# Seven block products for eight in a down projection, with sums of weights made in device memory

## The chip, the cores and the metric

The kernel runs on one core of one Trainium2 chip. The metric is the device time of one execution in microseconds (us). Before the change the median of three runs is 1150.55 us (1149.58 to 1152.34).

## The reference

One decoder layer is applied to a prompt of 512 rows and to 8 samples of 8 rows, 576 columns in the kernel's transposed layout. Model width is 1024. In order: a half-step feed-forward layer, a mixer (a recurrent branch and a pooling branch), cross attention over 256 memory tokens, a second half-step feed-forward layer, a final norm. All is float32. The part that changes is the second feed-forward step:

```python
def swiglu(x, w_gate, w_up, w_down):
    return (jax.nn.silu(x @ w_gate) * (x @ w_up)) @ w_down

x = x + 0.5 * swiglu(rmsnorm(x, p['ffn2_norm']), p['ffn2_w_gate'], p['ffn2_w_up'], p['ffn2_w_down'])
```

The hidden width is 2816, that is 22 chunks of 128.

## The kernel before

Activations are kept transposed: `x` is a tile of 128 partitions, 8 panels (the 1024 model channels) and 576 columns, cut in two halves of HT = 288 columns. It stays in SBUF from the first step to the last.

**Precision.** Each float32 operand is split into a high part (a cast to fp32r on ACT, line 144) and a low part (source minus high part on DVE, line 145). A product is three matmuls, high by high, high by low, low by high (`mm3`, line 159). With 128 x 128 weights and 288 columns each matmul is one entry of line 132 in the profile.

**Gate and up.** The function `ffn` (line 331) makes both steps. The first chunks of hidden channels (3 in step one, 2 in step two, `STD`) are plain products (`std`). For each further chunk f the gate and up weights and the two column halves are treated as 2 x 2 blocks and multiplied in the Strassen-Winograd way: seven products (named 11, E, 22, F, G, 12, H) for eight, with sums of the weights (DVE, lines 407, 408, 409, 420), sums of the activations made once (`HalfNorm.sums`, `last`), and sums of the results gathered in PSUM, with copies of partial results by ACT (lines 585, 589, 599). Each such product is 12 matmuls. Weights are loaded two chunks ahead (`load`, line 389) into a ring of four raw tiles (tag "wr"), and split in `prepare_a` and `prepare_b` into a ring of five (tags "wh", "wl").

**Hidden values.** A finished chunk of hidden values is split into `hh`, `hl` (lines 572 to 576), in groups of 4, 4, 4, 5, 5 chunks (`FGS`).

**Down.** While the chunks of one group are made, the down projection of the group before is worked off: `down` (line 448) puts steps in a queue, one for each output panel j and chunk k, six matmuls each (2 halves x 3). After each of the seven products of a chunk, `fill` (line 564) takes about 1.1 steps from the queue. When a panel's last chunk is done, DVE adds the PSUM tile to `x` (line 464). The down weights come in panels through the same ring "wr" and are split by `make` (line 436). The last group has no products left to lie beside: it runs as a tail, with columns cut 320 and 256 (`TAIL`, lines 653 to 676), and the final norm follows panel by panel.

**Order.** The order of the matmuls of both steps is written out by hand: inside the PSUM pool "ff" each matmul gets an edge to the one before (lines 130 to 138). The order of ACT, DVE, POOL and the DMA queue of SP is a planner's: it takes the instruction that comes first in the text among those it reckons to be ready. So the Silu of line 611 starts at 1041.50 us in the trace and the cast to "wh_g" at 1043.03, though the latter stands first in the text. On the chip each engine then runs its list in that order.

**PSUM.** "u" has two banks, "c" and "a" one each, "d" two tiles of two banks, which the down projection uses.

Of the kernel before, what the change touches and what calls it, by code (L numbers as in the profile page):

```python
# [9 lines left out]
F32 = mybir.dt.float32  # L10
# [6 lines left out]
P = 128  # L17
# [5 lines left out]
FGS = (4, 4, 4, 5, 5)  # L23
STD = (3, 2)
TAIL = ((0, 320), (320, T))
WARM = 11
# [39 lines left out]
def hybrid_step(ctx, tc, a):  # L66
# [60 lines left out]

    chain = [None]

    def mm(*args, **kw):  # L130

        i = te.matmul(*args, **kw)  # L132
        if "ff" in now:
# [4 lines left out]
        return i  # L138


# [189 lines left out]

    def ffn(name, n, fp, turn, plain, head=False):

        wstd, wgu, wd = a[f"{name}_s"], a[f"{name}_gu"], a[f"{name}_d"]

# [6 lines left out]
        def small_tile(nm_):  # L341
            return fp.tile([P, HT], F32, tag="pc", bufs=3, name=nm_)

        def full_tile(nm_):
            return fp.tile([P, T], F32, tag="e", bufs=2, name=nm_)

# [29 lines left out]
        def std_out(i, pg, pu):  # L376
            e = full_tile("e")
            for (p, q), (_, rr) in zip(pieces(pg, e), pieces(pg, r)):
                v.tensor_mul(q, p, rr)
            s.activation(e, e, AF.Silu, scale=-1.0)  # L380
            v.tensor_mul(e, e, half)
            for p, q in pieces(pu, e):
                v.scalar_tensor_tensor(out=q, in0=p, scalar=-1.0, in1=q, op0=ALU.mult, op1=ALU.mult)
            split(hh[0][:, i, :], hl[0][:, i, :], e)

# [36 lines left out]


        steps = deque()
        panels = [(gi, j) for gi in range(len(FGS)) for j in range(DC)]
        fetched, wdown = {}, {}

        def fetch(i):

            if i < len(panels) and i not in fetched:  # L430
                gi, j = panels[i]
                c0, fg = sum(FGS[:gi]), FGS[gi]
                fetched[i] = wp.tile([P, fg, P], F32, tag="wr", bufs=WRB, name=f"wr_d{j}")
                nc.sync.dma_start(fetched[i], wd[j, :, c0:c0 + fg, :])

        def make(i, pool=None):

            if i < len(panels) and i not in wdown:
                fetch(i)
                gi, j = panels[i]  # L440
                if pool is None:
                    w = [fp.tile([P, FGS[gi], P], F32R, tag=tag, bufs=2, name=f"{tag}{j}") for tag in ("dh", "dl")]
                else:
                    w = [pool.tile([P, FGS[gi], P], F32R, name=f"t{q}{j}") for q in "hl"]
                split(*w, fetched[i])
                wdown[i] = w

        def down(gi, after=None):

            fg = FGS[gi]  # L450
            h_, l_ = hh[gi], hl[gi]
            pd = {}

            def step(j, k):
                i = gi * DC + j
                if k == 0:
                    make(i)
                    make(i + 1)
                    fetch(i + 2)
                    pd[j] = dual("pd")  # L460
                mm3([pd[j][:, h, :HT] for h in range(2)], [q[:, k, :] for q in wdown[i]],
                    [[q[:, k, h * HT:(h + 1) * HT] for h in range(2)] for q in (h_, l_)], k == 0, k == fg - 1)
                if k == fg - 1:
                    v.tensor_add(halves(x[:, j, :]), pd[j][:, :, :HT], halves(x[:, j, :]))  # L464
                    if after:
                        after(j)

            steps.extend((step, j, k) for j in range(DC) for k in range(fg))

        def go(m):  # L470
            for _ in range(min(m, len(steps))):
                q, *at = steps.popleft()
                q(*at)

# [5 lines left out]

        group(0)
        ts = [fp.tile([P, 2, 3, HT], F32, tag=tag, bufs=2, name=f"t_{tag}") for tag in ("hh", "hl")]

# [53 lines left out]
        for i in range(3):  # L537
            s.copy(r[:, i * third:(i + 1) * third], free[i][:, HT:HT + third])
        half = fp.tile([P, T], F32, name=f"half_{n.name}")
        s.activation(half, r, AF.Copy, scale=0.5)  # L540
        std(cols(ps1[1]), w, range(4, DC))
        std_out(0, *ps0)
        load(plain)
        if plain > 2:
# [11 lines left out]
        load(plain + 1)  # L556
        prepare_b(plain)

# [5 lines left out]
        def fill():  # L564
            nonlocal pace
            if gi:
                pace += per_slot
                m = min(int(pace), len(steps))
                pace -= int(pace)
                go(m)  # L570

        def finish_chunk(c):
            w, U, g, h_, l_ = c
            product(U, w["22"], n, T4, False)
            v.tensor_mul(g[:, :HT], U, g[:, :HT])
            split(h_, l_, g)

        for f in range(plain, FFC):
            if f - g0 == FGS[gi]:
                g0, gi = f, gi + 1  # L580
                group(gi)
            w = W.pop(f)
            U, C, A = (single(tag, f"p{tag}")[:, :HT] for tag in "uca")
            product(U, w["11"], n, N11, True)
            s.copy(A, U)
            fill()
# [6 lines left out]
            if f == g0:  # L593
                down(gi - 1)
            prepare_a(f + 1)
            fill()
            product(U, w["F"], n, T2, False)
            u2 = small_tile("u2")
            s.copy(u2, U)
            fill()  # L600
# [3 lines left out]
            v.tensor_mul(g[:, HT:], g[:, HT:], r[:, HT:])  # L604
            fill()
            prepare_b(f + 1)
            if f == plain:
                n.last(0, ts[0][:, :, 0, :])
            product(A, w["12"], n, N21, False)
            v.tensor_mul(g[:, :HT], A, r[:, :HT])  # L610
            s.activation(g, g, AF.Silu, scale=-1.0)
            v.tensor_mul(g, g, half)
            fill()
# [3 lines left out]
            load(f + 2)  # L617
            if f == plain:
                n.last(1, ts[1][:, :, 0, :])
            if f == FGS[0] - 1:  # L620
                make(0)
                fetch(1)
            fill()
            before = w, U, g, hh[gi][:, f - g0, :], hl[gi][:, f - g0, :]
        finish_chunk(before)
        after = turn()
        if after:
# [3 lines left out]

        fg = FGS[-1]
        tp = now["tail"]
# [19 lines left out]
        for c0, c1 in TAIL:  # L653
            for j in range(DC):
                pd = single("u", "pd") if j % 2 else dual("pd")[:, 0, :]
                po = pd[:, :c1 - c0]
                for k in range(fg):
                    mm3([po], [q[:, k, :] for q in ws[j]], [[q[:, k, c0:c1]] for q in (hh[gi], hl[gi])],
                        k == 0, k == fg - 1)
                y = x[:, j, c0:c1]  # L660
                v.tensor_add(y, po, y)
                if j == 0:
# [32 lines left out]
    if True:  # L695
# [67 lines left out]
        def proj(kind, c):  # L763
            base = {"l": 0, "g": LC, "p": 2 * LC}[kind]
            ps[kind, c] = bank(f"in_{kind}{c}")
            project(ps[kind, c], panel(a["w_in"][base + c], DC, P, "i"), nm.xx)

        def lru_in(c):
# [407 lines left out]

    ffn("f2", n2, begin("f2", side="right"), to_tail, STD[1])
    end("f2", "tail", "ff")
# [10 lines left out]
def _inputs(i):  # L1189
# [43 lines left out]
    for n in (1, 2):  # L1233
# [5 lines left out]
        out[f"f{n}_gu"] = gu.reshape(FFC - m, P, 4, KP, P)[:, :, [3, 0, 1, 2]]  # L1239
        out[f"f{n}_d"] = panels(l0[f"ffn{n}_w_down"])  # L1240
    out["w_in"] = panels(l0["w_in"])
# [48 lines left out]
```

## Time and profile before

| what | value |
|---|---|
| median of three runs | 1150.55 us |
| the profiled execution's own time | 1148.76 us |
| its span | 1146.7 us |
| granted TensorE clock over the span | 0.997 |
| PE busy | 1129.4 us, 98% |
| DVE busy | 835.0 us, 73% |
| ACT busy | 544.0 us, 47% |
| POOL busy | 24.1 us, 2% |
| data moved | 126.30 MB, mean 110 GB/s |

The span runs from the first to the last instruction of the profiled execution; its own time holds what lies around the span too. Busy time of PE is to be read with care, since matmuls are pipelined; in the loops the interval from one matmul's start to the next is the better measure. An engine's idle time costs something only where the chain that ends last runs through it. The second step's chunk loop begins a little before 770 us and ends near 1098 us, the tail follows.

### The profile page before, as it was taken

The page shows a single profiled execution, that of the slowest core. Times are in us where ns is not written, and L with a number is a line of the kernel's source. Part 1 is how long each engine was busy: PE and PEld are TensorE (multiplying, and loading weights), DVE is VectorE, ACT ScalarE, POOL GpSimd, SP SyncE. Part 2 cuts the span into 40 slices and gives each one's busy share as a digit, 9 for nine tenths or more (in the row PEclk, how much of TensorE's full clock was granted, in tenths as well). Part 3 has the DMA queues.
Part 4 walks back from the last instruction along what each step waited for, and adds up shares of the span by engine and source line. Part 5 has one row for each costly group of instructions (what it writes and reads, how often), then busy time and mean ns, then how long its engine had stood idle before and what let it go on. Part 6 is the DMA issues. An engine that isn't in the chain of part 4 may idle for free.

```text
span 1146.7 us, 20764 instructions
## 1 busy us (share of the span) xinstructions
PE 1129.4 (98%) x8634; PEld 1113.0 (97%) x8634; DVE 835.0 (73%) x1335; ACT 544.0 (47%) x852; POOL 24.1 (2%) x47
## 2 busy tenths in 40 slices
PE   8999999999999999999999999999999999999996
PEld 8999999999999999999998879999999999999996
DVE  8887787788774788977634566769877877877664
ACT  8644344444432555875622564545443443443343
POOL 0000000000000022110000000000000000000000
PEclk9999999999999999999999999999999999999998
DMA  8223233233221352232655753212333332332212
GB/s 294 94 83 110 75 93 101 83 95 115 80 81 51 116 177 60 71 128 87 224 199 181 281 201 93 74 37 84 93 93 91 94 92 75 106 104 72 88 47 83
DMA packets 44285, 126.30 MB, mean 110 GB/s; under 512 B 4832, under 2 KB 9952, under 8 KB 44064
## 3 DMA queue, kind: packets, MB, share of 16 engines
q1 hardware_dynamic: 41808, 122.84, 34.4%
q10 hardware_dynamic: 2384, 2.15, 0.6%
q8 instruction: 67, 1.10, 0.4%
q14 instruction: 26, 0.21, 0.1%
HBM read 120.16 MB, written 4.81 MB: 109 GB/s over the span
## 4 chain that ended last, share of the span: by engine, by line
PE 94%; DVE 3%; ACT 1%; issue 1%; DMA 0%; DVEq 0%
PE pd L132 25%; PE pu L132 23%; PE pc L132 11%; PE pa L132 5%; PE q L132 5%; PE wo L132 5%; PE xo L132 4%; PE pg L132 3%; PE k L132 2%; PE v L1024 2%; PE in_l L132 2%; PE in_p L132 2%; PE o L132 1%; PE s L132 1%; PE puc L132 1%; PE ss L992 1%
## 5 line engine op out<-in xcount | busy, mean ns | idle before, releaser
L132 PE MATMUL pd<-hh,dl 128*128 128x288 f32 (+2 forms) x644 | 139.6, 295 | 0.0
L132 PE MATMUL pd<-hh,dh 128*128 128x288 f32 (+2 forms) x644 | 139.1, 295 | 0.0
L132 PE MATMUL pd<-hl,dh 128*128 128x288 f32 (+2 forms) x644 | 138.9, 294 | 0.0
L132 PEld LDWEIGHTS pd<-hh,dh 128*128 128x128 f32 x644 | 103.9, 188 | 0.0
L132 PEld LDWEIGHTS pd<-hh,dl 128*128 128x128 f32 x644 | 103.5, 188 | 0.1
L132 PEld LDWEIGHTS pd<-hl,dh 128*128 128x128 f32 x644 | 103.2, 188 | 0.0
L144 ACT CAST oh_b<-r 128x512 fp32r<-128x512 f32 x39 | 24.2, 621 | 119.6 <-PE pa L132 107.1
L144 ACT CAST wh_e<-r 128x1024 fp32r<-128x1024 f32 x39 | 41.0, 1052 | 63.0 <-PE pu L132 56.9
L144 ACT CAST dh<-wr_d 128x512 fp32r<-128x512 f32 (+1 forms) x74 | 48.7, 658 | 40.8 <-PE pd L132 29.9
L464 DVE TENSOR_TENSOR x<-pd,x 128x576 f32<-128x576 f32 x72 | 54.3, 754 | 18.1 <-PE pd L132 18.1
L145 DVE TENSOR_TENSOR wl_e<-r,wh_e 128x1024 fp32r<-128x1024 f32 x39 | 47.7, 1223 | 13.2 <-ACT wh_e L144 13.2
L144 ACT CAST wh_g<-r 128x1024 fp32r<-128x1024 f32 x39 | 41.1, 1055 | 33.0 <-DVE r L420 29.2
L145 DVE TENSOR_TENSOR dl<-wr_d,dh 128x512 fp32r<-128x512 f32 (+1 forms) x74 | 54.0, 730 | 0.0
L145 DVE TENSOR_TENSOR wl_g<-r,wh_g 128x1024 fp32r<-128x1024 f32 x39 | 47.7, 1224 | 7.3 <-ACT wh_g L144 5.4
L145 DVE TENSOR_TENSOR wl_a<-r,wh_a 128x1024 fp32r<-128x1024 f32 x39 | 47.6, 1220 | 3.4 <-ACT wh_a L144 3.0
L603 DVE TENSOR_TENSOR g<-pc,u 128x288 f32<-128x288 f32 x39 | 17.8, 457 | 40.9 <-PE pc L132 40.6
L132 PE MATMUL pu<-n2h,wl_a 128*128 128x288 f32 x160 | 47.4, 296 | 0.0
L132 PE MATMUL pu<-n2h,wh_a 128*128 128x288 f32 x160 | 47.4, 296 | 0.0
L132 PE MATMUL pu<-n2l,wh_a 128*128 128x288 f32 x160 | 46.8, 293 | 0.5 <-DVE n2l L145 0.5
L610 DVE TENSOR_TENSOR g<-pa,rstd_n 128x288 f32<-128x288 f32 x39 | 17.8, 457 | 39.8 <-PE pa L132 39.4
L144 ACT CAST wh_a<-r 128x1024 fp32r<-128x1024 f32 x39 | 40.9, 1050 | 8.8 <-PE xo L132 3.5
L132 PE MATMUL pu<-n1l,wh_a 128*128 128x288 f32 x152 | 44.8, 295 | 0.0
(496 smaller groups left out, 3682.0 us busy)
## 6 DMA issues: line engine op xcount, KB each, us to landing
r<-f_gu SPq DMA_DIRECT2D x78, 512.0 KB, 3.7
wr_d<-f_d SPq DMA_DIRECT2D x48, 256.0 KB, 2.8
wr_d<-f_d SPq DMA_DIRECT2D x32, 320.0 KB, 3.1
ck<-ck SPq DMA_DIRECT2D x16, 512.0 KB, 4.6
cv<-cv SPq DMA_DIRECT2D x16, 512.0 KB, 7.1
wr_i<-w_in SPq DMA_DIRECT2D x12, 512.0 KB, 3.7
wr_s<-f_s SPq DMA_DIRECT2D x8, 512.0 KB, 4.6
wr_o<-w_out SPq DMA_DIRECT2D x8, 512.0 KB, 3.6
```

Of the source, the lines that this page charges most:

```text
L132: i = te.matmul(*args, **kw)
L144: s.copy(hi, src)
L145: v.tensor_tensor(out=lo, in0=src, in1=f(hi), op=ALU.subtract)
L464: v.tensor_add(halves(x[:, j, :]), pd[j][:, :, :HT], halves(x[:, j, :]))
L603: v.tensor_add(g[:, HT:], C, u2)
L610: v.tensor_mul(g[:, :HT], A, r[:, :HT])
L992: te.matmul(sps[b * 32:(b + 1) * 32, g, :ML], lhsT=z[:, 4 * g + b, j, :], rhs=t[:, b, :], start=j == 0, stop=j == DC - 1)
L1024: te.matmul(ps[:, m, :HD], lhsT=lhs[:, kd, ms], rhs=w[wi][:, k, :], start=kd == 0 and i == 0, stop=kd == DC - 1 and i == 2)
```

## The change

In the second step (`fast=True`) the down projection of chunks 0 to 15 is now made in the Strassen-Winograd way too. The 16 chunks are four groups of four (`FAST = 4`). In each group, output panels go by twos (`NQ = 4` pairs). The blocks are: an output panel each, two chunks each, a half of the columns each. Seven products of 2 x 3 matmuls stand for eight. Chunks 16 and 17 (`PLAIN[0]`) keep the old form in the loop, chunks 18 to 21 (`PLAIN[1]`) are the tail, which was 17 to 21.

- Hidden values of a pair of chunks become seven operands each for high and low (`build_a`, `build_b`; tags "ph", "pl", three pairs).
- The down weights of a pair of panels come in one tile "td" (one buffer; two transfers) and one tile "t2" (`fetch_main`, `fetch_22`); `ensure` splits them in four parts into three buffers, and makes two sums on DVE.
- Each `fill` takes one entry of the queue: s11, sE, sF, s12, sH, and sG with s22 together. The results are gathered in four PSUM quarters U, C, A, D (both "d" tiles). ACT copies partial sums (A, D) and takes the parts out, times 0.5 or -0.5 (`take`), into SBUF tiles "acc" (one buffer) and "sq" (two). GpSimd then starts transfers that add these tiles to `x`. The plain panels 16 and 17 are added in this way as well; the factor 0.5, which was in `half`, moves there.
- Two sums of the down weights and two sums of each chunk's gate and up weights are made beforehand in device memory (`gsum`, `dsum`) by transfers that GpSimd starts during the first step and the mixer's projections: one copies two blocks, a second adds a third block to both. `background` sends them, each after the latest matmul emitted so far.
- So of the four sums of gate and up weights that DVE made for a chunk, two are left (`sum_g`). The gate and up parts are loaded in five transfers for two (`load_pairs`, `load_22`), and split at other places: `prepare_e`, `prepare_g`, `prepare_h`, `prepare_22`.
- Tiles of the second step: small tiles "pc" 2 for 3, full tiles "e" 3 for 2.

```diff
+FAST = 4
+PLAIN = (16, 2), (18, 4)
+NQ = DC // 2
...
+    jobs = deque()
+    for i in range(nfast):
+        w = a["f2_gu"][i].rearrange("p b k n -> p b (k n)")
+        jobs.append((gsum[i], w[:, 0:2, :], w[:, 3:4, :].to_broadcast([P, 2, KP * P])))
+        if i < FAST * NQ:
+            w = a["f2_d"][i // NQ, i % NQ].rearrange("p b k n -> p b (k n)")
+            jobs.append((dsum[i // NQ][i % NQ], w[:, 0:2, :], w[:, 3:4, :].to_broadcast([P, 2, 2 * P])))
+    added = deque()
+
+    def background(n=1):
+
+        for _ in range(min(n, len(jobs) + len(added))):
+            go_ = []
+            if len(added) > 1 or not jobs:
+                out, more = added.popleft()
+                go_.append(nc.gpsimd.dma_start(out, more, accum_op=ALU.add))
+            if jobs:
+                out, first, more = jobs.popleft()
+                go_.append(nc.gpsimd.dma_start(out, first))
+                added.append((out, more))
+            for i in go_:
+                tc.add_manual_dep(i.ins, latest[0].name, mybir.DependencyInfo(
+                    mybir.DependencyClass.Sync, mybir.DependencyReason.DATA), reason="pace")
...
+        def sum_g(f):
+            if f < FFC:
+                r0, r1 = raws[f]
+                v.tensor_add(r0[:, 1], r0[:, 1], r0[:, 0])
+                v.tensor_add(r0[:, 0], r0[:, 1], r1[:, 0])
...
+                if k == fg - 1 and fast:
+                    add = rows.tile([P, T], F32, tag="sq", name="add")
+                    s.activation(halves(add), pd[j][:, :, :HT], AF.Copy, scale=0.5)
+                    nc.gpsimd.dma_start(x[:, j, :], add, accum_op=ALU.add)
...
+        def build_a(p):
+
+            pair(p)
+            hi, lo = pairs[p]
+            t = halves(raw[2 * p])
+            b11, b12, b22 = t[:, 0, :], t[:, 1, :], raw[2 * p + 1][:, HT:]
+            t2[p] = small_tile("t2")
+            split(hi[:, N11, :], lo[:, N11, :], b11, -1.0)
+            v.tensor_sub(b11, b12, b11)
+            v.tensor_sub(t2[p], b22, b11)
+            v.tensor_sub(b12, b12, b22)
+            split(hi[:, T1:T3 + 1:2, :], lo[:, T1:T3 + 1:2, :], t)
+            split(hi[:, T2, :], lo[:, T2, :], t2[p])
+
+        def build_b(p):
+            (hi, lo), b2 = pairs[p], raw[2 * p + 1]
+            b21 = b2[:, :HT]
+            split(hi[:, N21:N22 + 1, :], lo[:, N21:N22 + 1, :], halves(b2), -1.0)
+            v.tensor_sub(b21, b21, t2[p])
+            split(hi[:, T4, :], lo[:, T4, :], b21)
...
+        def fetch_main(i):
+
+            if i < FAST * NQ:
+                g, q = divmod(i, NQ)
+                t = draw[i] = fp.tile([P, 4, 2, P], F32, tag="td", name=f"td{i}")
+                nc.sync.dma_start(t[:, 0:4:3], dsum[g][q].rearrange("p b (k n) -> p b k n", n=P))
+                nc.sync.dma_start(t[:, 1:3], a["f2_d"][g, q, :, 1:3])
...
+        def ensure(n):
+
+            while made[0] < min(n, 4 * FAST * NQ):
+                i, k = divmod(made[0], 4)
+                w = [fp.tile([P, 2, 2, P], F32R, tag=tag, bufs=3, name=f"{tag}{i}{k}") for tag in ("dh", "dl")]
+                t = draw[i]
+                if k == 3:
+                    split(*(q[:, 0] for q in w), draw.pop((i, 0)))
+                    fetch_22(i + 1)
+                else:
+                    if k:
+                        v.tensor_add(t[:, k], t[:, k], t[:, k - 1])
+                    split(*w, t[:, k:k + 2])
+                    if k == 2:
+                        fetch_main(i + 1)
...
+            def s11(i):
+                ensure(4 * i + 2)
+                d0, d1 = dual("d0"), dual("d1")
+                ps[i] = [t[:, h, :HT] for t in (d0, d1) for h in range(2)]
+                U, C, A, D = ps[i]
+                put(i, "11", N11, U, True)
+                s.copy(A, U)
+
+            def sE(i):
+                U, C, A, D = ps[i]
+                put(i, "E", T1, C, True)
+                t = halves(rows.tile([P, T], F32, tag="acc", bufs=1, name="add_e"))
+                take(t[:, 0, :], C, -1)
+                take(t[:, 1, :], C, 1)
+                j = 2 * (i % NQ)
+                nc.gpsimd.dma_start(x[:, j:j + 2, HT:], t, accum_op=ALU.add)
+
+            def sF(i):
+                ensure(4 * i + 3)
+                U, C, A, D = ps[i]
+                put(i, "F", T2, U, False)
+                s.copy(D, U)
+
+            def s12(i):
+                U, C, A, D = ps[i]
+                put(i, "12", N21, A, False)
+                ps[i, 1] = rows.tile([P, T], F32, tag="sq", name="add_1")
+                take(ps[i, 1][:, :HT], A, -1)
+
+            def sH(i):
+                ensure(4 * i + 4)
+                U, C, A, D = ps[i]
+                put(i, "H", T3, U, False)
+                ps[i, 2] = rows.tile([P, T], F32, tag="sq", name="add_2")
+                take(ps[i, 2][:, HT:], U, 1)
+
+            def sG(i):
+                ensure(4 * i + 5)
+                U, C, A, D = ps[i]
+                put(i, "G", N22, D, False)
+                t = ps.pop((i, 1))
+                take(t[:, HT:], D, -1)
+                nc.gpsimd.dma_start(x[:, 2 * (i % NQ), :], t, accum_op=ALU.add)
+
+            def s22(i):
+                U, C, A, D = ps[i]
+                put(i, "22", T4, U, False)
+                t = ps.pop((i, 2))
+                take(t[:, :HT], U, 1)
+                nc.gpsimd.dma_start(x[:, 2 * (i % NQ) + 1, :], t, accum_op=ALU.add)
+
+            for i in range(g * NQ, (g + 1) * NQ):
+                steps.extend([(q, i) for q in qs] for qs in ((s11,), (sE,), (sF,), (s12,), (sH,), (sG, s22)))
...
         def fill():
             nonlocal pace
-            if gi:
+            if fast:
+                go(1)
+            elif gi:
...
+            if fast and f in range(4, 4 * FAST + 1, 4):
+                quick(f // 4 - 1)
             product(U, w["F"], n, T2, False)
             u2 = small_tile("u2")
             s.copy(u2, U)
+            if fast:
+                sum_g(f + 1)
...
-                v.tensor_add(y, po, y)
+                if fast:
+                    v.scalar_tensor_tensor(out=y, in0=po, scalar=0.5, in1=y, op0=ALU.mult, op1=ALU.add)
+                else:
+                    v.tensor_add(y, po, y)
```

More of the change, by code (lines that the diff above doesn't have):

```diff
@@ L479, in group, with hidden @@
                 d[gi] = fp.tile([P, FGS[gi], T], F32R, tag=tag, bufs=2, name=f"{tag}{gi}")
-        group(0)
-        ts = [fp.tile([P, 2, 3, HT], F32, tag=tag, bufs=2, name=f"t_{tag}") for tag in ("hh", "hl")]
+        def hidden(f):
+            if fast:
+                b = 2 * (f % 2)
+                return [q[:, b:b + 2, :].rearrange("p h n -> p (h n)") for q in pairs[f // 2]]
+            gi = max(i for i in range(len(groups)) if groups[i][0] <= f)
+            return [q[gi][:, f - groups[gi][0], :] for q in (hh, hl)]
@@ new lines, in ffn, with pair @@
+        raw, raw22, pairs, t2 = {}, {}, {}, {}
+        def pair(p):
+            pairs[p] = [fp.tile([P, 7, HT], F32R, tag=tag, bufs=3, name=f"{tag}{p}") for tag in ("ph", "pl")]
+        def build_a(p):
[10 more added lines that the diff above has]
+            split(hi[:, T2, :], lo[:, T2, :], t2[p])
@@ new lines, in build_b, with build_plain @@
+        def build_b(p):
[4 more added lines that the diff above has]
+            split(hi[:, T4, :], lo[:, T4, :], b21)
+        def build_plain(f):
+            if f // 2 not in pairs:
+                pair(f // 2)
+            split(*hidden(f), raw[f])
+        draw, dparts, made = {}, {}, [0]
+        def fetch_main(i):
[4 more added lines that the diff above has]
+                nc.sync.dma_start(t[:, 1:3], a["f2_d"][g, q, :, 1:3])
@@ L630, in ffn @@
             return
[L632 removed]
+        g0, fg = groups[gi]
         tp = now["tail"]
```

201 lines of the change are left out of this document (165 added, 36 removed).

## The prediction

> **What bounds the kernel now.** I read the page first, then the busy time by stretches of the second step, the waits of TensorE, the groups of DVE and ACT with shapes kept apart, and the DMA issues.
>
> ```profile
> span 1146.7 us, 20764 instructions
> PE 1129.4 (98%) x8634; PEld 1113.0 (97%) x8634; DVE 835.0 (73%) x1335; ACT 544.0 (47%) x852; POOL 24.1 (2%) x47
> PE 94%; DVE 3%; ACT 1%; issue 1%; DMA 0%; DVEq 0%
> ```
>
> TensorE is busy for 98% of the span and is 94% of the chain that ended last. So a matmul removed shortens the program by its issue interval, as long as DVE and ACT keep up. The stretches below are the second step: its opening, four stretches of its chunk loop, the loop's end, the tail; the last row lies in the first step's loop.
>
> ```profile
> 764.00:800.00 36.00, 35.29 (x265) 34.72 (x264) 33.25 (x55) 21.85 (x35) 0.00 (x0) 1.00 0.18 52
> 800.00:870.00 70.00, 70.00 (x531) 70.00 (x530) 55.15 (x82) 28.47 (x44) 0.00 (x0) 1.00 0.30 91
> 870.00:940.00 70.00, 70.00 (x532) 70.00 (x531) 54.65 (x82) 28.88 (x44) 0.00 (x0) 1.00 0.31 92
> 940.00:1010.00 70.00, 70.00 (x532) 70.00 (x531) 54.12 (x80) 29.75 (x45) 0.00 (x0) 1.00 0.32 95
> 1010.00:1080.00 70.00, 70.00 (x532) 70.00 (x531) 54.29 (x81) 29.82 (x44) 0.00 (x0) 1.00 0.30 90
> 1080.00:1098.00 18.00, 18.00 (x138) 18.00 (x137) 7.77 (x14) 4.59 (x8) 0.00 (x0) 1.00 0.21 61
> 1098.00:1146.70 48.70, 39.07 (x296) 38.32 (x294) 26.40 (x58) 21.81 (x43) 0.00 (x0) 0.94 0.21 69
> 130.00:200.00 70.00, 70.00 (x532) 70.00 (x531) 55.18 (x82) 28.92 (x44) 0.00 (x0) 1.00 0.31 92
> ```
>
> Columns: stretch, length, busy us (and instructions) of PE, weight loads, DVE, ACT and POOL, granted clock, DMA share, GB/s. Three numbers matter. One matmul of 288 columns costs 70 / 532 = 0.1316 us. In the loop PE never stops with DVE at 54.6 / 70 = 78% and ACT near 29 / 70 = 42%. In the opening DVE stands at 33.25 / 36 = 92%, and even there PE loses only 0.71 us. The waits of PE from 760 us on agree:
>
> ```profile
> PE rs L132 <- DVE rf_f L238: 1.4, 1, 1.4
> PE pd L132 <- DVE x L661: 1.0, 2, 0.5
> PE pu L132 <- DVE n2l L145: 0.5, 1, 0.5
> PE pc L132 <- DVE e L383: 0.3, 1, 0.3
> ```
>
> **The change part by part.** *Matmuls.* A pair of output panels times four chunks was 2 x 4 x 3 x 2 = 48 matmuls and becomes 7 x 2 x 3 = 42. There are 4 groups x 4 pairs, so 16 x 6 = 96 go: 96 x 0.1316 = **12.6 us off**. The tail keeps four chunks in place of five, but what it loses the loop gains (chunks 16 and 17 run there in the old form), and 320 + 256 columns cost what twice 288 do. This is the whole gain, and it is PE's alone.
>
> *DVE.* The durations are these:
>
> ```profile
> L464 DVE TENSOR_TENSOR x<-pd,x 128x576 f32<-128x576 f32 x72 | 54.3, 754 | 18.1 <-PE pd L132 18.1
> L145 DVE TENSOR_TENSOR wl_g<-r,wh_g 128x1024 fp32r<-128x1024 f32 x39 | 47.7, 1224 | 7.3 <-ACT wh_g L144 5.4
> L145 DVE TENSOR_TENSOR dl<-wr_d,dh 128x512 fp32r<-128x512 f32 x48 | 32.8, 683 | 0.0
> L145 DVE TENSOR_TENSOR hl<-g,hh 128x576 fp32r<-128x576 f32 x39 | 29.4, 755 | 2.5 <-ACT hh L144 2.2
> L612 DVE TENSOR_TENSOR g<-g,half_n 128x576 f32<-128x576 f32 x39 | 29.3, 752 | 1.5 <-ACT g L611 1.5
> L408 DVE TENSOR_TENSOR r<-r,r 128x512 f32<-128x512 f32 x39 | 26.9, 691 | 1.2
> L604 DVE TENSOR_TENSOR g<-g,rstd_n 128x288 f32<-128x288 f32 x39 | 17.9, 458 | 1.3
> L148 DVE SCALAR_TENSOR_TENSOR n2l<-x,neg,n2h 128x576 fp32r<-128x576 f32 x8 | 6.5, 812 | 0.0
> L145 DVE TENSOR_TENSOR kk<-k,kk 128x256 fp32r<-128x256 f32 x8 | 3.4, 422 | 2.0 <-ACT kk L144 1.9
> L308 DVE SCALAR_TENSOR_TENSOR t_n<-x,neg,b_n 128x288 f32<-128x288 f32 x4 | 2.1, 514 | 0.0
> L310 DVE TENSOR_TENSOR t_n<-b_n 128x288 f32<-128x288 f32 x4 | 1.8, 454 | 0.0
> ```
>
> While the new products run (chunks 4 to 19), a chunk is on average 84 + 42 = 126 matmuls, 16.6 us, and DVE has in it: splits of gate and up weights as before, 3 x 1.224 + 0.69 = 4.36; two of the four sums left, 2 x 0.691 = 1.38 (the other two come summed from device memory); the gate and up arithmetic as before, 6 x 0.458 + 0.752 = 3.50; splits of the down weights, 14 blocks for 8, 3 x 0.683 + 0.422 = 2.47, and their two sums, 2 x 0.422 = 0.84; half of a pair's seven operands, (0.514 + 0.812 + 0.755 + 6 x 0.454) / 2 = 2.40. The adds of line 464 (0.754 each) are gone. Sum **14.95 us of 16.6, 90%**. Counted the same way the old loop comes to 4.36 + 4 x 0.691 + 3.50 + 0.755 + 1.88 panels (8 in 4.25 chunks) x (0.683 + 0.754) = 14.1 in 84 + 48 = 132 matmuls, 17.4 us, 81%, where the trace has 78%; so 86 to 90%.
>
> *ACT.* Its rows:
>
> ```profile
> L144 ACT CAST wh_g<-r 128x1024 fp32r<-128x1024 f32 x39 | 41.1, 1055 | 33.0 <-DVE r L420 29.2 <-PE pua L132 3.9
> L144 ACT CAST dh<-wr_d 128x512 fp32r<-128x512 f32 x48 | 29.8, 620 | 15.7 <-PE pd L132 13.3 <-DMA wr_d<-f_d 1.8
> L611 ACT ACTIVATE g<-g 128x576 f32<-128x576 f32 x39 | 26.8, 688 | 5.6 <-DVE g L610 5.6
> L144 ACT CAST hh<-g 128x576 fp32r<-128x576 f32 x39 | 26.2, 672 | 18.2 <-DVE g L575 18.2
> L599 ACT COPY u<-pu 128x288 f32<-128x288 f32 x39 | 15.6, 400 | 30.6 <-PE pu L132 30.6
> L144 ACT CAST wh<-wr 128x256 fp32r<-128x256 f32 x8 | 2.9, 397 | 0.0
> ```
>
> Per chunk: casts of weights 3 x 1.055 + 0.62 = 3.79; three copies 1.20; Silu 0.69; down weights 3 x 0.62 + 0.40 = 2.26; the eight new copies out of PSUM (two partial sums, six parts of the answer) 8 x 0.40 = 3.20; hidden operands (3 x 0.40 + 2 x 0.672) / 2 = 1.27. Sum **12.4 of 16.6, 75%**, from 42%. Neither engine is full, so the count alone costs nothing. What they cost is lateness. Bound from below: 0, as in the loop at 78%. From above: the opening's loss at 92%, 0.71 us in 36, over 16 x 16.6 = 266 us: 5.2 us. At 86 to 90% I take nearer the upper row: **+3**.
>
> *The handover between panel pairs.* The last product of a pair is followed, after one chunk product of 12 x 0.1316 = 1.58 us, by the first product of the next pair in the same two PSUM tiles; before that ACT must copy out the last part. 0.40 fits, but not behind a cast of 1.055 and a second copy (1.86). Twelve handovers lie inside groups: 0 to 12 x 0.28 = 3.4; a cast stands there only part of the time, I take **+0.5**. The copies A and D have two slots, some 4 us, and are free.
>
> *Additions into x by transfer.* They take the place of DVE's adds and are waited for by nobody in the loop unless the two "sq" tiles come back late: from the issue after step sG to the same tile's next writing, s12 of the next pair, lie about 10 us of PE work (four chunk products, three and a half steps). Transfers of this size here:
>
> ```profile
> r<-f_gu SPq DMA_DIRECT2D x78, 512.0 KB, 3.7
> wr_d<-f_d SPq DMA_DIRECT2D x48, 256.0 KB, 2.8
> cv<-cv SPq DMA_DIRECT2D x16, 512.0 KB, 7.1
> x<-xT SPq DMA_DIRECT2D x8, 288.0 KB, 4.8
> o_v<-vo ACTq DMA_DIRECT2D x4, 256.0 KB, 8.5
> ```
>
> No accumulating transfer is in the trace. From 2.8 to 8.5 us, all within 10: **0**, with the upper end close (a rival below).
>
> *Sums in device memory.* 20 x 1024 KB and 16 x 512 KB, 28.7 MB, in the first step and the mixer's projections, some 365 us: 79 GB/s beside 92, DMA share from 0.31 to at most 0.7 if an addition costs double. Loads that then land in 7.1 us for 3.7 are still there, a chunk of 17 us ahead: **0**, bounds 0 and +3 (3.4 us once). POOL has only its small copies of the mixer to delay.
>
> *Opening and tail.* Two sums less per chunk where DVE is fullest, but one pair's operands more: of the 0.71 lost there I take back **-0.3**. In the tail, fewer steps cover the last split (one step and nine matmuls, about 2.1 us, for a chain of 0.46 + 0.67 + 0.755 us and its hand-offs), and two "sq" tiles come out of transfers: 0 to +1.5, taken **+0.5**.
>
> *Sum.* -12.6 + 3 + 0.5 - 0.3 + 0.5 = -8.9. The profiled execution took 1148.76 us (span 1146.7 and 2.06 around it); 1148.76 - 8.9 = 1139.9. The median of the three runs, 1150.55, lies 1.8 higher: **1141.7, say 1141.5**.
>
> **The rivals.** *A, the single buffer of down weights decides: slower.* Tile "td" holds one pair's weights. The next may be fetched only after the third split of this pair, and step s11 of the next needs their first split. At the place in the code that is 78 matmuls, 10.3 us. Along the chain lie 0.42 + 0.62 + 0.68, a transfer of 3.7 to 7.1, 0.62 + 0.68: 6.7 to 10.1, and up to four queue positions behind a 1.2 us operation: to 14.9. At 2.3 us late, the middle of the excess, twelve handovers cost 27 us: about 1168. It decides from 0.9 us per handover. Against it: the planner can take the third split earlier by up to two steps, 4.7 us.
>
> *B, the additions into x come late.* POOL makes these requests, and its work is delayed beside DVE:
>
> ```profile
> 418.56 0.19 POOL L773 COPY small<-u 128x3 f32<-128x3 f32 x1 [10.77 <-DVE u L737]
> 424.36 2.02 POOL L773 COPY small<-u 128x3 f32<-128x3 f32 x1 [0.46 <-DVE u L737]
> 424.42 1.21 DVE L145 TENSOR_TENSOR wl_i<-wr_i,wh_i 128x1024 fp32r<-128x1024 f32 x1
> ```
>
> The same copy took 0.19 us alone and 2.02 beside DVE, and DVE's own split kept its 1.21. With 8.5 + 2.0 + 0.4 = 10.9 us ACT would wait 0.9 us per pair, 13 us in all: 1155.
>
> [...]
>
> *C, DVE is full in effect.* The new splits hand work from DVE to ACT and back up to five times a pair; 2 us more idling per chunk brings 14.95 to 17, over PE's 16.6: half to all of the gain is gone, 1146 to 1153. The opening speaks against it.
>
> *D, the sums disturb the first step, or the change moves matmuls without removing any exposed time*: 1150.
>
> **Numbers.** Forecast 0.61 with its own range 1137 to 1147; A 0.15, B 0.08, C 0.12, D 0.04. A measurement of this kernel tells 0.2%, 2.3 us, from no change. Faster: 0.61 and half of C, 0.67; same: the rest of C near 1150 and half of D, 0.07; slower: A, B and what is left, 0.26. The range 1137 to 1160 takes in B, C, D and the beginning of A.
>
> **What would show it.** PE's matmuls down by 96, busy time by about 12.6 us; DVE at 86 to 90% and ACT near 75% between chunks 4 and 19; PE waiting some 3 to 4 us there, in pieces under 1 us, on ACT's copies and DVE's splits. A: waits of PE on "dl" behind transfers into "td", near 2 us each. B: ACT waiting for POOL's transfers before "add_1". C: DVE above 95%. D: idle PE before 430 us. A gain beyond 13.5 us, or PE idle over 10 us in the loop, proves the sum wrong.

## The result and the profile after

The changed kernel takes 1144.22 us (median of five runs, 1143.38 to 1144.31) and the kernel before 1150.54 us beside it (five runs, 1148.43 to 1152.34). The ratio is 0.9945, 95% interval 0.993 to 0.9959: faster by 0.4 to 0.7%. The forecast was 1141.5 us.

The page of the changed kernel, its first lines and the chain that ended last:

```profile
span 1142.4 us, 21333 instructions
PE 1121.4 (98%) x8538; PEld 1103.8 (97%) x8538; DVE 833.8 (73%) x1391; ACT 610.9 (53%) x1051; POOL 132.1 (12%) x175
PE 92%; DVE 4%; ACT 2%; issue 1%; DMA 1%; DVEq 0%; ACTq 0%
```

The 96 matmuls are gone (8634 to 8538). PE's busy time fell by 8.0 us, not by 12.6, and the span by 4.3 (1146.7 to 1142.4). So some 8 us of the gain came back somewhere. The stretches of the second step and one of the first, with the columns of the prediction's table, say where:

```profile
764.00:800.00 36.00, 33.05 (x238) 32.61 (x237) 31.94 (x57) 20.65 (x35) 0.00 (x0) 0.95 0.25 74
800.00:870.00 70.00, 70.00 (x531) 69.96 (x529) 57.83 (x99) 46.76 (x94) 11.94 (x12) 1.00 0.67 161
870.00:940.00 70.00, 70.00 (x528) 69.77 (x527) 57.22 (x100) 47.28 (x96) 12.35 (x13) 1.00 0.71 176
940.00:1010.00 70.00, 70.00 (x529) 69.86 (x528) 57.19 (x100) 46.99 (x94) 12.72 (x13) 1.00 0.71 177
1010.00:1080.00 70.00, 70.00 (x530) 69.96 (x529) 49.14 (x80) 42.88 (x87) 13.29 (x14) 1.00 0.68 152
1110.00:1126.00 16.00, 15.48 (x112) 15.28 (x111) 6.54 (x19) 8.93 (x18) 0.00 (x0) 0.89 0.00 1
130.00:200.00 70.00, 70.00 (x532) 70.00 (x531) 54.92 (x81) 28.69 (x44) 10.35 (x14) 1.00 0.67 163
```

- *Opening (764 to 800).* 238 matmuls against 265: 27 x 0.1316 = **3.6 us lost**. The granted clock, 1.00 before, is 0.95 over the stretch and 0.50 from 785.97 to 789.09 us, where a matmul of 288 columns comes every 0.24 us and not every 0.13.
- *Loop (800 to 1080).* 531 + 528 + 529 + 530 = 2118 matmuls against 2127: 9 x 0.1316 = **1.2 us lost**, spread over 280 us.
- *First step (130 to 200).* 532 as before, although DMA share went from 0.31 to 0.67.
- *The rest.* -4.3 = -12.6 + 3.6 + 1.2 + 3.5: that leaves some **3.5 us** that came back after 1080 us, at the loop's end and in the tail.

The waits of PE from 740 us on:

```profile
PE pu L136 <- ACT n2h L178: 2.2, 1, 2.2
PE pd L136 <- DVE acc_f L969: 1.4, 1, 1.4
PE rs L136 <- DVE rf_f L272: 1.4, 1, 1.4
PE pu L136 <- DVE n2l L179: 0.7, 1, 0.7
PE pd L136 <- DVE x L960: 0.5, 1, 0.5
PE pu L136 <- DVE e L903: 0.2, 1, 0.2
PE pd L136 <- DVE pl L179: 0.2, 1, 0.2
```

The first and the fourth, 2.9 us, stand in the opening, on the operand `n2h`, `n2l` of the product "22" of the first chunk made in the Strassen-Winograd way. That operand is the last sum of the activations (`n.last(1)`). Before, PE waited 0.5 us there. What DVE did ahead of it, from its timeline:

```profile
770.68 0.45 DVE L182 SCALAR_TENSOR_TENSOR pl<-e,ph 128x288 fp32r<-128x288 f32 x1
...
771.65 0.46 DVE L587 TENSOR_TENSOR e<-e 128x288 f32<-128x288 f32 x1
...
774.59 1.13 DVE L179 TENSOR_TENSOR pl<-e,ph 128x576 fp32r<-128x576 f32 x2
775.63 0.46 DVE L884 TENSOR_TENSOR g<-pc,u 128x288 f32<-128x288 f32 x1
...
780.66 0.52 DVE L352 SCALAR_TENSOR_TENSOR t_pl<-x,cst,n2h 128x288 f32<-128x288 f32 x1
...
784.82 0.77 DVE L179 TENSOR_TENSOR n2l<-t_pl,n2h 128x576 fp32r<-128x576 f32 x1
```

Lines 182, 587 and 179 with "pl" are the operands of the first pair of chunks (`build_a(0)`, `build_b(0)`). They run from 770.68 to 775.7 us, ahead of the sum (lines 352 and 179 with "n2l") that PE then stands waiting for. Nobody needs those operands so early. The first matmul that reads them, from PE's timeline, starts 16 us later than the first one behind that wait:

```profile
784.54 0.40 PE L136 MATMUL pu<-n2h,wh 128*128 128x288 f32 x1 [2.25 <-ACT n2h L178]
...
800.63 0.29 PE L136 MATMUL d<-ph,dh 128*128 128x288 f32 x1
```

The transfers that the change adds, with the median time to landing in the last column:

```profile
gsum<-f_gu POOLq DMA_DIRECT2D x40, 512.0 KB, 8.6
x<-add POOLq DMA_DIRECT2D x40, 288.0 KB, 4.4
dsum<-f_d POOLq DMA_DIRECT2D x32, 256.0 KB, 5.8
x<-add_e POOLq DMA_DIRECT2D x16, 288.0 KB, 6.5
```

### The profile page after: what moved, and what is told of

The parts are those of the page before. It is cut to its first block, busy times and chain, and to the rows that moved or that the text cites. A ratio compares the mean times of both kernels' runs of the same rounds, so it can differ in the third digit from the quotient of the medians.

```text
span 1142.4 us, 21333 instructions
## 1 busy us (share of the span) xinstructions
PE 1121.4 (98%) x8538; PEld 1103.8 (97%) x8538; DVE 833.8 (73%) x1391; ACT 610.9 (53%) x1051; POOL 132.1 (12%) x175
## 4 chain that ended last, share of the span: by engine, by line
PE 92%; DVE 4%; ACT 2%; issue 1%; DMA 1%; DVEq 0%; ACTq 0%
PE pu L136 22%; PE pd L136 16%; PE pc L136 10%; PE d L136 8%; PE pa L136 5%; PE q L136 5%; PE wo L136 4%; PE xo L136 4%; PE pg L136 3%; PE k L136 2%; PE v L1326 2%; PE in_l L136 2%; PE in_p L136 2%; PE o L136 1%; PE s L136 1%
## 5 line engine op out<-in xcount | busy, mean ns | idle before, releaser
L136 PE MATMUL pd<-hh,dl 128*128 128x288 f32 x352 | 75.3, 295 | 0.0
L136 PE MATMUL pd<-hh,dh 128*128 128x288 f32 x352 | 75.1, 294 | 0.0
L136 PE MATMUL pd<-hl,dh 128*128 128x288 f32 x352 | 75.0, 294 | 0.0
L136 PE MATMUL d<-ph,dh 128*128 128x288 f32 x224 | 66.7, 298 | 0.0
L136 PE MATMUL d<-ph,dl 128*128 128x288 f32 x224 | 66.3, 296 | 0.0
L136 PE MATMUL d<-pl,dh 128*128 128x288 f32 x224 | 66.1, 295 | 0.0
L136 PEld LDWEIGHTS pd<-hh,dl 128*128 128x128 f32 x352 | 56.3, 188 | 0.0
L136 PEld LDWEIGHTS pd<-hh,dh 128*128 128x128 f32 x352 | 56.3, 188 | 0.0
L136 PEld LDWEIGHTS pd<-hl,dh 128*128 128x128 f32 x352 | 56.1, 188 | 0.0
L136 PE MATMUL pu<-n1l,wh_a 128*128 128x288 f32 x152 | 44.9, 295 | 0.0
L136 PE MATMUL pu<-n1h,wl_a 128*128 128x288 f32 x152 | 44.8, 295 | 0.0
```

## The experiments

**The changed kernel once more**, as the partner of the next two.

> The changed kernel once more, as the measure for the three beside it. Every theory: 1143.4 to 1144.3 us, ratio to the kernel before 0.994 to 0.995, PE losing some 4.7 us between 764 and 800 us of the span and about 1.2 us between 800 and 1080 us.

1145.5 us (1143.38 to 1146.17), ratio 0.9956 [0.9941, 0.9971]: 1.3 us above the first five runs, and 4.3 below the kernel before beside it (1149.82). So a median of this kernel can move by more than 1 us. Its trace has the same opening: 238 matmuls, clock 0.95, waits of 2.2 and 0.7 us.

**The operands of the first pair later.** Nothing but the place of two calls:

```diff
-            build_a(0)
-            build_b(0)
...
+                if fast:
+                    build_a(0)
+                    build_b(0)
```

They stood before the first chunk's products; now they stand behind `n.last(1)` in the first product-form chunk.

> The seven operands of the first pair of chunks are made behind the last operand of the norm, no longer ahead of it. Theory 1, that their 4.8 us on DVE ahead of that operand are what makes PE wait in the opening: the wait of 2.25 and 0.70 us for n2h and n2l at 782 us falls to below 1 us in all, the half clock that follows it goes (1.5 us), and the time falls by 2.5 to 3.7 us against the changed kernel, to about 1141. Rival, that DVE is simply full there and any order loses the same: the wait turns up at another operand in the next 20 us, and the time stays within 1 us of the changed kernel.

1140.02 us (1137.29 to 1140.36), ratio 0.9907 [0.989, 0.9923], 5.5 us below the run beside it and 4.2 below the changed kernel's first five runs. The same kernel once more:

> The kernel with the first pair's operands made late, once more, as the measure for the two that undo a part of the change beside it. Every theory: 1139 to 1141 us, no wait of PE over 0.3 us between 764 and 1090 us.

1139.87 us (1138.44 to 1141.0), ratio 0.9905 [0.989, 0.992]. The opening and one stretch of the tail of this second run:

```profile
764.00:800.00 36.00, 36.00 (x276) 36.00 (x275) 32.98 (x57) 24.20 (x43) 0.00 (x0) 1.00 0.33 98
1110.00:1126.00 16.00, 15.48 (x106) 15.28 (x106) 6.87 (x18) 7.00 (x14) 0.00 (x0) 0.79 0.01 3
```

276 matmuls for 238, that is 38 x 0.1316 = 5.0 us: more than the 3.6 that the change had lost there. The waits on `n2h` and `n2l` are gone, and the clock is 1.00. The order on DVE was the cause, not its load: DVE is busier here (32.98 of 36) than in the changed kernel (31.94). The opening can also be measured from its first matmul into "pu" to the first one of the down projection. These two are, in the changed kernel (the second is shown above, at 800.63) and here:

```profile
760.86 0.43 PE L136 MATMUL pu<-n2h,wh_s 128*128 128x288 f32 x2
...
760.80 0.43 PE L136 MATMUL pu<-n2h,wh_s 128*128 128x288 f32 x2
...
795.50 0.29 PE L136 MATMUL d<-ph,dh 128*128 128x288 f32 x1
```

That is 39.77 us against 34.70, 5.07 less. In the kernel of the next experiment, which has the same wait but the full clock behind it, it is 38.25. So 1.5 of the 5.07 us is the half clock and 3.5 the wait, which is more than the 2.9 us of idling: in the changed kernel the starts of three matmuls in a row lie at 782.00, 784.54 and 785.64 us, 3.64 us for two intervals that are 0.26 elsewhere, so 3.4 more. I had expected 2.5 to 3.7 us in all, the half clock included, and allowed for up to 1 us of wait that would stay; none stayed. In the tail, the second line of the first table, this execution ran at a clock of 0.79, and that of the run before at 1.00.

**The tail's norm one panel earlier.** The last 256 columns' panels overlap the final norm of the first 320:

```diff
-                if c0 and j == 1:
+                if c0 and j == 0:
...
-                if c0 and j == 4:
+                if c0 and j == 3:
```

> The row factor and the scaling of the first 320 columns are written one output panel earlier in the tail. Theory 2, that the tail of four chunks leaves less cover for DVE's 3.0 us of scaling, and so for the last sum of squares: the wait of 1.38 us on acc_f falls to about 0.5, the time by 0.5 to 1 us against the changed kernel, and by up to 1.5 us more if the half clock in the tail goes with the moved matmuls. Rival, that the row factor is not ready so early: PE waits for it at its new place instead, up to 1 us, and the time stays within 0.5 us.

1144.53 us (1141.6 to 1146.48), ratio 0.995 [0.9932, 0.9969]: 1.0 us below the changed kernel beside it, but with ranges that overlap, so no change is shown. Its opening and its waits in the tail:

```profile
764.00:800.00 36.00, 33.05 (x250) 32.60 (x249) 33.23 (x59) 20.54 (x35) 0.00 (x0) 1.00 0.25 74
...
PE pd L136 <- DVE x L960: 1.0, 2, 0.5
PE pd L136 <- DVE x L948: 0.7, 1, 0.7
```

The wait of 1.4 us for "acc_f" is gone, but "x" takes its place twice (0.5 more, and a new 0.7): the earlier sums now stand where PE has nothing else to do. The first line gives something that I had not looked for: the same busy time of PE as in the changed kernel (33.05 us), the same two waits, but clock 1.00 and 250 matmuls for 238. So the half clock that followed the wait in the two traces of the changed kernel is worth 12 x 0.1316 = 1.6 us, and after the same wait it came twice and once did not.

**Both edits.**

> Both of these edits. If both theories hold the gains add: 3 to 5 us below the changed kernel, 1139 to 1141. If theory 1 alone holds: the time of the run with late operands, about 1141. If neither: 1143.4 to 1144.3.

1139.55 us (1137.31 to 1139.98), ratio 0.9903 [0.9887, 0.9919]: like the first edit alone. The second adds nothing that can be told.

**PE kept busy in the opening's wait.** In the changed kernel, 24 matmuls are written into the product "22" (the trace has 48) which read the identity and write columns of the PSUM tile "pa" that no product uses; everything else is kept. They share a PSUM bank with a partial sum, and the values of the output differ from those of the changed kernel; the work of the other instructions is the same.

```diff
+            if spare is not None and k == 2:
+                for _ in range(24):
+                    mm(spare, lhsT=ident, rhs=ident, start=True, stop=True, skip_group_check=True)
...
-            product(U, w["22"], n, T4, False)
+            spare = full[2][:, HT:HT + P] if fast and len(W) == 2 else None
+            product(U, w["22"], n, T4, False, spare)
```

> The changed kernel with 24 extra matmuls of 128 columns into unused PSUM columns, put where PE waits in the opening. The wait for the operand stays as it is. Theory 4, that the half clock in the opening of the changed kernel comes from PE's idling and costs some 1.5 us on top of the wait: the granted clock between 764 and 800 us is 1.00 and 12 more matmuls of the 288 columns fall in that stretch (250 for 238); the time is 0 to 1.6 us below the changed kernel, 1142.5 to 1145. Rival, that the clock falls for another reason: 0.95 there, as before.

1144.41 us (1143.43 to 1145.27), ratio 0.9949 [0.9935, 0.9962]. The opening, PE's added matmuls as a group, and the tail:

```profile
764.00:800.00 36.00, 36.00 (x283) 36.00 (x283) 31.67 (x57) 20.60 (x36) 0.00 (x0) 1.00 0.25 74
...
L136 PE MATMUL pa<-ident 128*128 128x128 f32 x48 | 5.5, 275 | 0.0
...
1110.00:1126.00 16.00, 15.48 (x111) 15.28 (x111) 6.61 (x19) 9.16 (x18) 0.00 (x0) 0.89 0.01 2
```

With PE never idle the clock stays at 1.00 in the opening, while in the tail, where nothing was altered, it falls to 0.89 as before. The fill is longer than the hole: it holds PE for 5.5 us where 2.9 stood empty, so 283 - 48 = 235 real matmuls fit against 238, and the time is the same. That the clock follows PE's idling is not settled by this. Over the whole span the clock lay at 0.993 or 0.994 in all eleven executions of the changed kernel and at 0.994 to 0.996 in the four of this one, which fits. But in the kernel with the earlier norm, whose wait stays empty, the clock of the opening was 1.00 too in the one trace. A gain in time was not shown.

**All sums on DVE.** From here on the kernels start from the one with the late operands (1140 us). Here no sums are made in device memory; DVE makes all four of a chunk's gate and up weights, and all four of a pair of down panels:

```diff
-        for _ in range(min(n, len(jobs) + len(added))):
+        for _ in range(0):
...
-... (e[:, 0], w[:, 1], w[:, 2], e[:, 1])):
+... (w[:, 0], w[:, 1], w[:, 2], w[:, 3])):
...
+                v.tensor_add(r0[:, 0], r0[:, 0], r1[:, 1])
+                v.tensor_add(r1[:, 1], r1[:, 1], r0[:, 1])
...
-... dsum[g][q].rearrange("p b (k n) -> p b k n", n=P))
+... a["f2_d"][g, q, :, 0:4:3])
...
+                    if k == 0:
+                        v.tensor_add(t[:, 0], t[:, 0], t[:, 3])
+                        v.tensor_add(t[:, 3], t[:, 3], t[:, 1])
```

> Late operands, and no sums made beforehand in device memory: the weights come as they are, and DVE makes all four sums of a chunk's gate and up weights and all four of a pair of down panels. The output is the same sums in another place. That adds 2 x 0.69 + 2 x 0.42 = 2.2 us of DVE to the 57.3 / 70 x 16.7 = 13.7 us that it is busy per chunk, 15.9 of 16.7 us, 95%. Theory 3, that lateness costs little up to about 90% and grows close to full: 2 to 8 us slower than the kernel with late operands, with waits of PE on DVE's splits, and the first step as before (531 matmuls in 70 us with or without the transfers). Rival, that the sums beforehand buy nothing: within 0.5 us of it.

1174.03 us (1173.16 to 1175.3), ratio 1.0207 [1.0193, 1.0221]: **34 us slower** than with the sums in device memory, where I had put 2 to 8. One stretch of its loop and DVE's waits for transfers between 800 and 1080 us:

```profile
940.00:1010.00 70.00, 63.26 (x463) 61.31 (x462) 57.86 (x105) 41.62 (x85) 12.02 (x12) 1.00 0.62 145
...
DVE td L634 <- DMA td<-f_d: 24.2, 10, 4.7
DVE r L479 <- DMA r<-f_gu: 18.7, 11, 4.0
```

PE makes 463 matmuls for 529, and DVE is busy for 57.86 of 70 us (54.8 in the two stretches before), as in the changed kernel (57.2 to 57.8). It is not full; it waits for tiles that are not there yet, some 43 us of the 280. To see which of the two tiles it is, each kind of sum was made on DVE alone.

> Beside the kernel with late operands and all sums in device memory (1140.0 us), this one makes only the two sums of each pair of panels' down weights on DVE (32 more additions of 0.42 us, 13.4 us of DVE's time over 16 pairs of panels); the gate and up sums stay in device memory. The kernel that made both kinds on DVE took 34 us more, with DVE waiting 26.7 us for transfers into td and 18.7 us for transfers into r between 800 and 1080 us. Theory 1, the single buffer td: the first split now needs all of td, DVE stands waiting for it in order, and that is the larger part: 17 to 30 us slower, about 1157 to 1170, DVE waiting 20 us or more for td. Theory 2, the late second tile of gate and up weights is the cause and td's waits only follow from it: less than 8 us slower, under 1148. Theory 3, the two waits only cost when they stand one behind the other on DVE: under 8 us here and in the run beside this too.

1153.81 us (1152.02 to 1155.03), ratio 1.0028 [1.0017, 1.004]: 13.8 us above 1140, between what the first theory had and what the two others had.

```profile
940.00:1010.00 70.00, 67.42 (x498) 65.89 (x497) 55.58 (x100) 43.01 (x90) 11.92 (x12) 1.00 0.67 164
...
DVE td L631 <- DMA td<-f_d: 29.1, 14, 4.2
```

> The other half: only the two sums of each chunk's gate and up weights are made on DVE (40 more additions of 0.69 us, 27.6 us of DVE's time, 22 us of it in the loop, which brings DVE from 82 to about 90%); the down sums stay in device memory. Theory 1, the buffer td: 5 to 12 us slower than 1140, about 1145 to 1152, as the wait for r costs less than that for td; theory 2, the late second tile: 20 to 34 us slower, 1160 to 1174, with DVE waiting 18 us or more for r; theory 3: under 8 us slower. By the rate of loss at a full DVE alone (4 us in 210 at 92%) about 4 us.

1173.66 us (1171.17 to 1177.54), ratio 1.0207 [1.018, 1.0234]: 33.7 us above 1140.

```profile
940.00:1010.00 70.00, 61.68 (x441) 59.83 (x440) 55.33 (x98) 40.87 (x84) 11.90 (x12) 0.98 0.61 144
...
DVE r L478 <- DMA r<-f_gu: 44.9, 15, 6.1
```

My first theory, that the single buffer "td" costs most, falls: with the gate and up sums on DVE alone the kernel is 33.7 us slower, with the down sums alone 13.8, with both no more than 34. They are not additive, and neither are the waits in the rows above: 29.1 us for "td" alone and 44.9 for "r" alone, but 24.2 + 18.7 = 42.9 with both. That the longer delay leaves time in which the other transfer lands would fit, but no run shows it directly. It is not DVE's work alone either: the gate and up sums are 27.6 us of additions, and DVE's busy share did not rise.

What DVE stands in front of differs. The gate and up sums need the second tile of weights, r1, where the first split had needed r0 only. In one chunk of that trace r0's transfers are issued at 909.4 us and r1's at 911.9, and DVE waits for 3.3 us until the sum starts at 918.87. The down sums need nothing of "td" that was not needed before, since the first split reads a block of each of the two transfers in either form. But with the sums from device memory it is ACT's cast that comes first, and it waits for "td" for 1.4 us between 800 and 1080 us; now DVE's additions come first and wait for 29.1 us. For the gate and up weights, too, the first to need the transfer is now DVE and no longer ACT. How much the later tile costs and how much the change of engine was not separated.

**All additions into x by DVE.** The six parts of a pair go from PSUM into `x` by DVE, with no copies by ACT into "acc" and "sq" and no transfers; the sums in device memory stay:

```diff
+            def into(dst, src, sign):
+                v.scalar_tensor_tensor(out=dst, in0=src, scalar=0.5 * sign, in1=dst, op0=ALU.mult, op1=ALU.add)
...
-                nc.gpsimd.dma_start(x[:, j:j + 2, HT:], t, accum_op=ALU.add)
+                into(x[:, j, HT:], C, -1)
+                into(x[:, j + 1, HT:], C, 1)
```

and so for the parts out of A, U, D.

> Late operands, and the six parts of each pair's answer added into x by DVE straight from PSUM, without ACT's copies out and GpSimd's transfers (the two plain panels keep theirs). DVE gets 6 x 0.51 = 3.1 us per chunk, 13.7 + 3.1 = 16.8 of 16.7 us: full; ACT loses 2.4 us. Theory 3: DVE sets the pace between chunks 4 and 19, 5 to 20 us slower than the kernel with late operands. Rival, that PE only needs DVE's adds in time and the planner finds room: within 2 us of it.

1144.31 us (1143.16 to 1145.06), ratio 0.9947 [0.9935, 0.996]: 4.4 us slower than with the transfers, just under the lowest that I had expected. Three stretches and the one wait in them:

```profile
800.00:870.00 70.00, 69.26 (x521) 68.80 (x519) 64.68 (x125) 38.94 (x70) 0.00 (x0) 1.00 0.39 116
870.00:940.00 70.00, 68.60 (x514) 68.14 (x515) 64.27 (x121) 38.07 (x68) 0.00 (x0) 1.00 0.40 120
940.00:1010.00 70.00, 68.94 (x518) 68.42 (x517) 63.81 (x122) 37.84 (x68) 0.00 (x0) 1.00 0.38 116
...
PE d L136 <- DVE x L654: 3.2, 6, 0.7
```

DVE stands at 64 / 70 = 92%, and PE makes 521 + 514 + 518 = 1553 matmuls where the kernel with late operands makes 525 + 529 + 529 = 1583: 30 x 0.1316 = 3.9 us in 210. So the transfers into `x` are worth about 4 us here.

## Why the prediction was right, and where its terms were not

The forecast of a faster kernel held, and the time lies 2.7 us above 1141.5. By the profiled executions alone it held less well: the sum said -8.9 and the own time went from 1148.76 to 1144.22, -4.5. The 1.8 us by which the median before lay above its profile had been added to the forecast; after, profile and median are equal, and that made up 1.8 of the 4.4. That was luck; what the 1.8 was no run shows. The repeat beside its own partner moved by 4.3 us, where the forecast had 9.0.

| step of the sum | predicted | measured |
|---|---|---|
| 96 matmuls | -12.6 | 96 gone, interval 0.132 where PE does not wait |
| lateness in the loop, and the handover | +3.5 | +1.2 |
| additions into x, sums in device memory | 0 | 0: PE waits for neither in the loop |
| opening | -0.3 | **+3.6** |
| tail and the loop's end | +0.5 | **about +3.5** |

- **Matmuls.** The term stands: 529.5 matmuls in 70 us of loop are 0.1322 us each, against 0.1316.
- **Loop.** Oversized. DVE stood at 57.4 / 70 = 82% in the first three stretches and ACT at 47 / 70 = 67%, against 86 to 90 and 75. The durations of the rows overcount: in DVE's timeline above an instruction begins before the one ahead of it ends (774.59 + 1.13 is 775.72, and the next began at 775.63). The prediction saw that its own count gave 81% where the old trace had 78%, and took off too little. The rate that it took from the opening, 0.71 us in 36 at 92%, comes to 4.1 in 210; the kernel with additions on DVE lost 3.9 in 210 at 92%. The numbers agree, but that is not the same loss twice: in the kernel with the late operands DVE stands at 92% in the opening as well (32.98 of 36), and PE loses nothing there. That speaks for the order as the cause of the 0.71 too, though that kernel differs from the one before in more than the order. PE's waits of 3 to 4 us in pieces did not appear between 800 and 1080 us.
- **Opening.** Here is the step that failed: "two sums less per chunk where DVE is fullest, but one pair's operands more: of the 0.71 lost there I take back -0.3". It weighed amounts of DVE's work. The pair's operands stand ahead of the last sum of the activations in the text, and DVE ran them ahead of it (from 770.68 us on, the sum from 780.66); so it is their place that counts. Moving them was worth 4.2 to 5.5 us in the time and 5.07 us in the trace.
- **Tail.** Undersized. The 3.5 us can be placed: the waits for "acc_f" and "x", 1.4 + 0.5 against 1.0 before, +0.9; and a stretch of half clock, 112 matmuls in 1110 to 1126 us where the kernel with the additions on DVE, whose tail is the same, has 124 at clock 1.00: 12 x 0.129 = 1.5. The waits for "e" and "pl" of 0.2 each, new at the loop's end and the tail's start, cost 0.7 in the intervals of PE's timeline. And from the start of the last group of matmuls (1134.12 us for 1138.85 before) to the end of the span it is 8.28 us for 7.85, another 0.4. That makes up the 3.5.
- **Rival A**, the single buffer "td": absent from the changed kernel, where PE has no wait on "dl" between 800 and 1080 us. A late "td" does cost time, 13.8 us when DVE's additions stand in front of it, but not by the path of rival A: PE then waits for ACT's copies out of PSUM (5.1, 2.0 and 1.2 us between 800 and 1080 us) and not on "dl". With the sums from device memory no DVE instruction of the loop waits for a transfer; the prediction had priced these sums as DVE's time only.
- **Rival B**: ACT waited for none of POOL's transfers. They land in 4.4 and 6.5 us, within the 10 us window, and POOL's request takes 1.2 us in the row below, the longest of the four in the loop (0.9 to 1.2); those that make the sums before it took 1.0 to 1.1. A delay near 2 us did not show. In the prediction's rows the copy of 0.19 us did not run alone either: in that trace DVE's line 736 was at work from 418.55 to 419.00 us. So that DVE holds up POOL's requests was an estimate from the one copy of 2.02.
- **Rival C**: DVE is not full (57.4 of 70 us). **Rival D**: the first step has its 532 matmuls in 70 us with 163 GB/s as with 92, and the second step's first matmul into "pu" starts at 760.86 us for 760.97 before.

```profile
L668 POOL DMA_DIRECT2D x<-add_e x16 | 19.3, 1203 | 384.8 <-ACT dh L178 352.4 <-ACT add_e L651 32.5
```

The fastest kernels found are those with the late operands, 1139.6 to 1140.0 us: 0.8 to 1.1% below the kernel before, by their intervals.

## What to carry to other kernels

Where a change puts new work on an engine ahead of an operand that the bounding engine waits for, look at its place in the order and not at its share of the busy time: here two calls in the wrong place cost some 5 of the 12.6 us, at an unchanged load. Sums of weights that are made early in device memory saved little arithmetic on the path and much waiting: with all sums on DVE that engine waited some 43 us of 280 for loads, in the changed kernel for none there; price a removed operation by what it had to wait for as well. After the gap of 2.9 us on TensorE the clock was halved for a while in two of the three traces that have the gap, which cost another 1.5 us in the opening here; so close such a gap rather than count it.

## What the runs showed of the hardware

**Half the clock after a gap, sometimes.** In the tail of the changed kernel, from the timeline of PE (start, duration):

```profile
1116.51 0.28 PE L136 MATMUL pd<-ph,dl 128*128 128x256 f32 x1
1117.31 0.38 PE L136 MATMUL pd<-ones,acc_f 128*128 128x1 f32 x2 [0.52 <-DVE x L960]
...
1119.44 0.28 PE L136 MATMUL pd<-ph,tl 128*128 128x256 f32 x1
1119.56 0.28 PE L136 MATMUL pd<-ph,th 128*128 128x256 f32 x1
...
1120.46 0.42 PE L136 MATMUL pd<-pl,th 128*128 128x256 f32 x1
1120.68 0.42 PE L136 MATMUL pd<-ph,tl 128*128 128x256 f32 x1
...
1123.80 0.28 PE L136 MATMUL pd<-ph,tl 128*128 128x256 f32 x1
1123.91 0.29 PE L136 MATMUL pd<-ph,th 128*128 128x256 f32 x1
```

Between 1116.5 and 1119.1 us PE has only a wait and matmuls of one column. A matmul of 256 columns then comes every 0.12 us, from about 1120.2 us on every 0.21 us, and after some 3.4 us every 0.12 again; the granted clock is 0.50 from 1120.26 to 1123.45 us. In two executions of the kernel with late operands the same place ran once at full clock and once at half clock for 6.9 us, from 1113.8 to 1120.7 us; from these one-column matmuls to the last group of matmuls the second took 3.1 us longer. Ahead of the slow stretches stand 2.9 us of idling in two pieces in the opening and 2.6 us with tiny matmuls in the tail. What starts such a stretch, what sets its length and why it does not always come was not shown.

**Transfers that add.** Adding 288 KB to a tile in SBUF took 4.4 us to landing (x40) and 6.5 us where the tile's target is two half panels (x16), both medians. 512 KB in device memory took 8.6, copies and additions together. In the same trace plain loads on SP's queue took 4.8 us for 288 KB into `x` (x8) and, by kind, 3.9 to 5.1 us for the 256 KB pieces of "r" and "td" (x132). A plain transfer started by GpSimd into a tile in SBUF is not in the trace, so what the adding itself costs was not shown.
